# A diffusion transformer's first phase: three modulation mixtures move from TensorE to GpSimd and to the head of the queue

## The chip, the cores and the metric

The kernel runs on one core of a Trainium2 chip. The metric is the device time of one execution in microseconds (us), from the first to the last instruction with the little that lies around them; the time before is the median of three executions. TensorE is called PE here, VectorE DVE, ScalarE ACT, GpSimd POOL and SyncE SP, as in the profile. SP does no arithmetic in this kernel: it issues most of the transfers, in its program order, so that a transfer whose buffer isn't free holds up all that stand behind it.

## The reference, cut to what matters

The kernel computes a two-layer backbone. Layer 0 is a neighbourhood attention followed by a mixture of experts, layer 1 a bidirectional RWKV-7 mixing followed by another mixture of experts. Width is 1024, with 512 latent and 256 context tokens. Every layer is steered by six modulation vectors (shift, scale and gate for the mixer, the same for the experts):

```python
def ada_modulation(cond, w, b):
    m = jax.nn.silu(cond) @ w + b
    return jnp.split(m, 6, axis=-1)
```

`w` is 1024 x 6144 float32 for each layer, so each of the twelve modulations reads a 4 MB slice of weights and multiplies it with one or two vectors (`c` for the latent tokens and `c_ctx` for the context tokens). The three that the change touches, j = 3, 4, 5 of layer 1, steer the last mixture of experts, which is used for latent tokens alone.

## The kernel before, in words

Four phases follow one another: layer 0's attention (0 to about 500 us), its experts (to about 1190), the RWKV mixing (to about 2130), the last experts (to the end). The change lies in the first phase, `phase_na`.

**Start.** Six 128-row tiles of tokens are loaded and normalised, TensorE turns them to channels-first form (`raw`), and the two modulations j = 0 and 1 of layer 0 are computed. Then, for each of 8 chunks of channels k and for two column ranges (512 latent, 256 context), ACT writes the modulated tokens rounded to a shorter format, `hTh` (L563), and DVE writes the modulated tokens in full (`raw`, L564) and what the rounding lost, `hTl` (L566). These 32 DVE instructions are called the hTl chain here. At the same time POOL clears the two `kl` tiles (L230) and makes the attention masks `mR` with six selects (L237).

**The weave.** From then on a generator interleaves three lists of steps: the attention of one pair of heads (`na_attend`: scores L362, L363 and mask L372; softmax; transposes L80; values L411), the projection of the next pair (`na_project`: products in three passes L262, L263, L264 with weights `wraw` loaded by SP at L275, rounded by ACT to `wh` at L254, and the rest taken by DVE to `wl` at L255; POOL copies half of `kT` at L327), and the remaining modulations, `mods`, by `ADA` steps for each pair of heads, 33 of 40 in all. The other 7 steps run at the end, beside the last attention steps. The programming layer then orders each engine's queue by its own rules; each engine, and each queue of transfers, works strictly in order.

**One modulation, `ada(S, l, j)`.** Four steps. Each loads 256 rows of weights, 1 MB, into a buffer `adaw` (L129, SP, two buffers). TensorE multiplies: 8 matmuls of 128x256 by the vector's 32-column tile `sT` (L133; columns 0 and 1 carry the two vectors), and in the first step 4 small matmuls that add the bias `adab` (L138; loaded by POOL's queue at L126). DVE copies (L140) or adds (L142) the sum into `adam`. After four steps two transposes (L80) and a DVE copy (L147) write the column form `modT`. `adam` and `adab` have two buffers each.

Every float32 matmul appears as two records in the trace, so a step's 8 matmuls are 16 records of L133.

The order of the modulations was layer 0, j = 2 to 5, then layer 1, j = 0 to 5.

Of the kernel before, what the change touches and what calls it, by code (L numbers as in the profile page):

```python
# [20 lines left out]
F32 = mybir.dt.float32  # L21
# [5 lines left out]
ALU = mybir.AluOpType  # L27
# [4 lines left out]
P = 128  # L32
D = 1024
# [17 lines left out]
def vap(ap, dims, offset=0):  # L51
    return bass.AP(tensor=ap.tensor, offset=ap.offset + offset, ap=dims)
# [25 lines left out]
def transpose(S, out, in_):  # L78
    n = in_.shape[0]
    S.nc.tensor.transpose(out, in_, S.ident[:n, :n])  # L80
# [37 lines left out]
    S.modT = [cp.tile([P, 48, 2], F32, name=f"modT{l}") for l in range(2)]  # L118


def ada(S, l, j):

    nc, I = S.nc, S.I
    acc = S.small.tile([P, 256], F32, name="adam")
    adab = S.small.tile([24, 256], F32, name="adab")
    nc.gpsimd.dma_start(adab, I["ada_b"][l].rearrange("(c n) -> c n", n=256))  # L126
    for k in range(0, KD, 2):
        w = S.adaw.tile([P, 2, D], F32, name="adaw")
        nc.sync.dma_start(w, I["ada_w"][l, k * P:(k + 2) * P, j * D:(j + 1) * D].rearrange("(i p) n -> p i n", p=P))  # L129
        ps = S.ps_mm.tile([P, 512], F32, name="mm")[:, :256]  # L130
        for i in range(2):
            for q in range(4):
                nc.tensor.matmul(ps[32 * q:32 * q + 32], S.sT[:, k + i, :], w[:, i, q * 256:(q + 1) * 256],  # L133
                                 start=i == 0, stop=i == 1 and k > 0)
        if k == 0:
            for q in range(4):
                c = 4 * j + q
                nc.tensor.matmul(ps[32 * q:32 * q + 32], S.ident[0:24, c:c + 1].to_broadcast([24, 32]),  # L138
                                 adab, start=False, stop=True)
            nc.vector.tensor_copy(acc, ps)  # L140
        else:
            nc.vector.tensor_tensor(acc, ps, acc, op=ALU.add)  # L142
        yield
    pt = S.ps_tp.tile([P, 4, P], F32, name="tp")
    for s in range(2):
        transpose(S, pt[:, s, :], acc[:, s::2] if l == 1 and j in (3, 4) else acc[:, s * P:(s + 1) * P])
    nc.vector.tensor_copy(S.modT[l][:, 8 * j:8 * j + 8, :].rearrange("p (q s) w -> p s q w", s=2),  # L147
                          pt[:, 0:2].rearrange("p s (q r) -> p s q r", r=32)[:, :, :, 0:2])
# [73 lines left out]
def na_consts(S, pool):  # L222
    nc = S.nc
    S.mL = pool.tile([P, P], BF16, name="mL")
    nc.vector.memset(S.mL, 0.0)
    nc.vector.tensor_copy(S.mL[0:16].rearrange("m (c r) -> m c r", r=GR),
                          S.ident[0:16, 0:16, None].to_broadcast([16, 16, GR]))
    S.kl = [pool.tile([P, 2, 768], F32R, name=f"kl{i}") for i in range(2)]
    for i in range(2):
        nc.gpsimd.memset(S.kl[i].bitcast(F32), 0.0)  # L230
    S.mR = []
    for t in range(3):
        m = pool.tile([P, 32, GR], BF16, name=f"mR{t}")
        nc.vector.memset(m, 0.0)

        def sel(lo, hi, base, cm, step):
            nc.gpsimd.affine_select(out=m[0:16, lo:hi, :], in_=m[0:16, lo:hi, :],  # L237
                                    pattern=[[step, hi - lo], [0, GR]], compare_op=ALU.is_ge,
                                    fill=NEG, base=base + step * lo, channel_multiplier=cm)
        if t == 0:  # L240
            sel(0, 32, 8, -1, 1)
            sel(16, 32, 7, 1, -1)
        elif t == 1:
            sel(0, 32, 0, -1, 1)
            sel(0, 32, 15, 1, -1)
        else:
            sel(0, 16, -8, -1, 1)
            sel(0, 32, 23, 1, -1)
        S.mR.append(m)
# [17 lines left out]
def split_weights(S, pool, tag, sources, bufs):  # L267

    nc = S.nc
    out = []  # L270
    for h in range(2):
        raw = S.wraw.tile([P, 4, 256], F32, name="wraw")
        for c, src in sources:
            n = src.shape[1]
            nc.sync.dma_start(raw[:, :, c:c + n], src[h * 512:(h + 1) * 512].rearrange("(k p) n -> p k n", p=P))  # L275
        wh = pool.tile([P, 4, 256], F32R, name=f"{tag}h", bufs=bufs)
        wl = pool.tile([P, 4, 256], F32R, name=f"{tag}l", bufs=bufs)
        split(S, wh, wl, raw)
        out.append((wh, wl))
    return lambda k: tuple(w[:, k % 4, :] for w in out[k // 4])  # L280


def na_project(S, p, hT, wp, grp, Q):

# [3 lines left out]
    def product(w, t):  # L288
        ps = S.ps_mm.tile([P, 2, 256], F32, name="mm")
        for i in range(2):  # L290
            s = slice((t + i) * P, (t + i + 1) * P)
            passes(S, ps[:, i, :], [(hTh[:, k, s], hTl[:, k, s]) + w(k) for k in range(KD)])
            yield ps
    Q.q = grp.tile([P, 2, 768], F32R, name="qT")
    Q.k = grp.tile([P, 2, 768], F32R, name="kT")
    Q.kl = S.kl[p % 2]
    Q.BT = grp.tile([P, 2, 265], F32, name="BT")
    for s in range(2):
        nc.sync.dma_start(Q.BT[:, s], vap(S.rp, [[1, 16], [31, 8], [1, 265]], 465 * (2 * p + s)))
    w = split_weights(S, wp, "w", [(i * P, W[:, i * D + p * P:i * D + (p + 1) * P]) for i in range(2)], 3)  # L300
# [218 lines left out]
def phase_na(S):  # L519
    nc, tc, I = S.nc, S.tc, S.I  # L520
    with ExitStack() as es:
        pool = es.enter_context(tc.tile_pool(name="na", bufs=1))
# [34 lines left out]
        for j in range(2):  # L557
            for _ in ada(S, 0, j):
                pass
        cols = [mod_cols(S, 0, w, 0) for w in range(2)]  # L560
        for k in range(KD):
            for (a, b), sl in zip(cols, (slice(0, 512), slice(512, 768))):
                nc.scalar.activation(hTh[:, k, sl], raw[:, k, sl], AF.Identity, scale=a[:, k:k + 1], bias=b[:, k:k + 1])  # L563
                nc.vector.tensor_scalar(raw[:, k, sl], raw[:, k, sl], a[:, k:k + 1], b[:, k:k + 1],  # L564
                                        op0=ALU.mult, op1=ALU.add)
# [3 lines left out]
        grp = ea.enter_context(tc.tile_pool(name="nag", bufs=2, side="right", reuse_waits="tile"))  # L569
        att = ea.enter_context(tc.tile_pool(name="naa", bufs=1, side="right", reuse_waits="tile"))  # L570
        na_consts(S, att)
        Q = [Ctx() for _ in range(8)]

        def modulation():
            for l, js in ((0, range(2, 6)), (1, range(6))):
                for j in js:
                    yield from ada(S, l, j)
        def attention():
            for p in range(8):
                yield from na_attend(S, p, Q[p], Q[p - p % 2].V, Q[p - p % 2].VS, OT)  # L580

        def some(gen, n):
            for _ in range(n):
                next(gen, None)
                yield
        mods, att = modulation(), attention()
        weave(1, (na_project(S, 0, (hTh, hTl), wp, grp, Q[0]), 0, 1))
        for p in range(7):
# [1329 lines left out]
def phase_rw(S):  # L1918
    nc, tc = S.nc, S.tc
    S.rwk = ExitStack()  # L1920
    with ExitStack() as es:
        pool = es.enter_context(tc.tile_pool(name="rw", bufs=1))
        with ExitStack() as e1:
            if S.first == 3:
                with tc.tile_pool(name="adat", bufs=4) as S.adaw:
                    S.small = S.adaw
                    for j in range(6):
                        for _ in ada(S, 1, j):
                            pass
            S.small = e1.enter_context(tc.tile_pool(name="smallr", bufs=2))  # L1930
            rw_consts(S, pool)
            rw_inputs(S, pool)
# [4 lines left out]
        with ExitStack() as e1:  # L1937
# [56 lines left out]
            for k in range(n + LAG + 1):  # L1994
                j = k - LAG
# [47 lines left out]
def build(tc, I, out, upto=99, dbg=None, xin=None, first=1):  # L2043
    with ExitStack() as ctx:
# [28 lines left out]
        if upto >= 3:  # L2073
            R = phase_rw(S)
            if upto == 3:
                R.es.close()
# [40 lines left out]
```

## Time and profile before

| | |
|---|---|
| median of three runs | 2639.2 us (2630.35 to 2642.72) |
| profiled execution, its own time | 2646.59 us |
| its span, first to last instruction | 2644.8 us |
| PE busy, share of the span | 2400.1 us, 91% |
| DVE | 1275.4 us, 48% |
| ACT | 982.8 us, 37% |
| POOL | 555.3 us, 21% |
| mean granted TensorE clock | 0.954 of full speed |

A share is an average over four phases. The stretch of the first phase has to be read by itself, and within it three things: who waits for whom on PE, what each record of the modulations costs there, and what DVE and POOL do at the same moments. Where the trace shows a group such as "x16", the time beside it runs from the first start to the last end of the group. "[0.38 <-PE mm L264]" at the end of a row is idle time of that engine before the instruction and what ended it; "SPq" is SP's queue, and the time there is that of issuing, not of the transfer. In a line with three durations these are the shortest, the median and the longest, in ns.

### The profile page before, as it was taken

Reading aid. Unit: us, or ns where it says so; the run is one execution under the profiler, and the core shown is the slowest. Engines: PE = TensorE matmul, PEld = TensorE weight load, DVE = VectorE, ACT = ScalarE, POOL = GpSimd, SP = SyncE. Lnnn points to the kernel's source line nnn. Section 1 sums busy time; section 2 is a strip of 40 time slices with the busy share of each in tenths; the row PEclk is TensorE's granted clock in tenths of the full one; section 3 lists DMA queues with packets and bytes.
Section 4 is the critical chain, followed back from the end, with each engine's and each line's share of the span. In section 5 each row is a group of like instructions: output and inputs, shape, how many; then the busy total and the mean of one; then the engine's idle time right before and its main releaser. Section 6 shows DMA issues by size and latency. Waiting matters only on the chain. (4 is left out here: it accounts for less than half of the span.)

```text
span 2644.8 us, 43708 instructions
## 1 busy us (share of the span) xinstructions
PE 2400.1 (91%) x16800; PEld 1565.9 (59%) x16800; DVE 1275.4 (48%) x2997; ACT 982.8 (37%) x2057; POOL 555.3 (21%) x831
## 2 busy tenths in 40 slices
PE   5999999988999999996997979999999959998887
PEld 3988888783333433334896868777778843332232
DVE  5666666552222322339777445767666751222122
ACT  3566565431111111114676435666664421011010
POOL 2110100120000000005354055556565200000000
PEclk9999999998999999998997988989998959999999
DMA  6344444437989999863678665565553189999998
GB/s 249 99 130 143 139 131 137 163 147 294 409 352 365 367 350 378 320 239 121 184 244 281 172 137 117 127 131 130 128 125 97 59 333 403 420 421 420 420 421 342
DMA packets 402334, 637.59 MB, mean 241 GB/s; under 512 B 133220, under 2 KB 300448, under 8 KB 377552
## 3 DMA queue, kind: packets, MB, share of 16 engines
q1 hardware_dynamic: 395200, 613.30, 66.3%
q0 software_dynamic: 6928, 21.51, 2.2%
q8 instruction: 133, 2.18, 0.3%
q14 instruction: 73, 0.60, 0.1%
HBM read 565.11 MB, written 53.88 MB: 234 GB/s over the span
## 5 line engine op out<-in xcount | busy, mean ns | idle before, releaser
L823 PE MATMUL P<-wm,xin 128*64 128x512 f32 x2048 | 469.5, 601 | 25.6 <-DMA wm<-in_moe_w_dram 24.3
L823 PEld LDWEIGHTS P<-wm,xin 128*64 128x64 f32 x2048 | 140.4, 137 | 318.6 <-issue 251.3
L869 PE MATMUL mm<-wm,hidT 128*64 128x512 f32 x1024 | 233.7, 604 | 9.2 <-ACT hidT L856 7.1
L879 DVE SCALAR_TENSOR_TENSOR Y<-mm,gates,gt 64x512 f32<-64x512 f32 x64 | 48.0, 750 | 329.4 <-PE mm L869 328.7
L841 ACT ACTIVATE hid<-P 128x512 f32<-128x512 f32 x32 | 19.1, 597 | 443.9 <-PE P L823 443.9
L798 POOL DMA_INDIRECT xg<-xnd,ii x20 | 19.1, 953 | 775.9 <-PE tp L80 718.1
L262 PE MATMUL mm<-wh,hTh 128*128 128x256 f32 x576 | 168.1, 292 | 2.1 <-ACT hTh L563 2.1
L264 PE MATMUL mm<-wh,hTl 128*128 128x256 f32 x576 | 166.3, 289 | 1.6 <-DVE hTl L566 1.6
L263 PE MATMUL mm<-wl,hTh 128*128 128x256 f32 x576 | 165.8, 288 | 0.0
L869 PEld LDWEIGHTS mm<-wm,hidT 128*64 128x64 f32 x1024 | 71.1, 138 | 154.6 <-issue 134.8
L1648 POOL TENSOR_TENSOR Wi<-Wi,Ti 112x30 f32<-112x30 f32 (+14 forms) x240 | 141.7, 591 | 18.8
L1646 POOL TENSOR_TENSOR Ti<-Wi 112x30 f32<-112x30 f32 (+14 forms) x240 | 136.8, 570 | 18.2
L842 DVE TENSOR_TENSOR hid<-P,hid 128x512 f32<-128x512 f32 x32 | 22.1, 692 | 243.4 <-PE P L823 228.3
L832 PE MATMUL Pc<-wm,xin 128*32 128x512 f32 x1024 | 118.2, 603 | 0.0
L1725 PE MATMUL mm<-FR,QF 128*128 128x128 f32 (+1 forms) x768 | 117.5, 299 | 0.4 <-ACT QF L1713 0.4
L262 PEld LDWEIGHTS mm<-wh,hTh 128*128 128x128 f32 x576 | 110.7, 192 | 8.2 <-issue 5.7
L264 PEld LDWEIGHTS mm<-wh,hTl 128*128 128x128 f32 x576 | 110.6, 192 | 4.3 <-DVE hTl L566 2.7
L263 PEld LDWEIGHTS mm<-wl,hTh 128*128 128x128 f32 x576 | 110.7, 192 | 2.6 <-issue 2.5
L1725 PEld LDWEIGHTS mm<-FR,QF 128*128 128x128 f32 x768 | 101.0, 204 | 7.4 <-ACT QF L1713 0.9
L1713 ACT ACTIVATE QF<-mm 64x256 f32<-64x256 f32 x192 | 72.6, 378 | 69.3 <-PE mm L1709 65.6
L1728 DVE TENSOR_TENSOR FT<-mm,eye 64x128 f32<-64x128 f32 x192 | 55.9, 292 | 82.5 <-ACT FT L1727 80.4
L1742 PE MATMUL ch<-Z,FT 128*64 128x64 f32 x704 | 81.5, 241 | 9.2 <-DVE Z L1745 7.5
(445 smaller groups left out, 5542.1 us busy)
## 6 DMA issues: line engine op xcount, KB each, us to landing
wm<-in_moe_w_dram SPq DMA_DIRECT2D x382, 1024.0 KB
adaw<-in_ada_w_dram SPq DMA_DIRECT2D x48, 1024.0 KB
wraw<-in_na_w_qkv_dram SPq DMA_DIRECT2D x32, 256.0 KB
pkd<-sig SPq DMA_DIRECT2D x24, 256.0 KB
pkd<-kka SPq DMA_DIRECT2D x24, 256.0 KB
pkd<-av SPq DMA_DIRECT2D x24, 256.0 KB
sig<-pkd SPq DMA_DIRECT2D x16, 384.0 KB
kka<-pkd SPq DMA_DIRECT2D x16, 384.0 KB
```

The lines of the kernel that those rows point to most:

```text
L262: S.nc.tensor.matmul(ps, xh, wh, start=(k == 0), stop=False)
L263: S.nc.tensor.matmul(ps, xh, wl, start=False, stop=False)
L264: S.nc.tensor.matmul(ps, xl, wh, start=False, stop=(k == n - 1))
L823: S.nc.tensor.matmul(ps[64 * hf:64 * hf + 64], T.xl[:, k, T.cl], w[:, hf * 512:(hf + 1) * 512], start=k == 0, stop=k == KD - 1)
L832: S.nc.tensor.matmul(T.Pc[32 * i:32 * i + 32], T.xc[:, k, T.cc], w[:, (i % 2) * 512:(i % 2 + 1) * 512], start=k == 0, stop=k == KD - 1)
L869: S.nc.tensor.matmul(py[64 * hf:64 * hf + 64], T.hT[:, k % 4, k // 4, :], weights(R, "moe_w2", T.e, k)[:, hf * 512:(hf + 1) * 512], start= ...
L1646: nc.gpsimd.tensor_tensor(t, W3[:, i + 1:32, i:i + 1].to_broadcast([112, n, i]), W3[:, i:i + 1, 0:i].to_broadcast([112, n, i]), op=ALU.mult)
L1648: nc.gpsimd.tensor_tensor(W3[:, i + 1:32, 0:i], W3[:, i + 1:32, 0:i], t, op=ALU.add)
L1713: nc.scalar.activation(QF[m][0:64, u], pq[64 * u:64 * u + 64], AF.Copy)
L1725: nc.tensor.matmul(pf[:, h, s0:], QF[m][:, u, h, :], rhs, start=True, stop=True)
L1728: nc.vector.tensor_tensor(F[64:128, :, 64:128], pf[64:128, :, 64:128], S.eye2[64:128, None, :].to_broadcast([64, 2, 64]), op=ALU.add)
L1742: nc.tensor.matmul(pz[64:128, h, :], FT[m][u][:, h, 64:128], Zs[m][:, u, 64 * h:64 * h + 64], start=True, stop=True)
```

## The change

For layer 1, j = 3, 4, 5, POOL takes each 128-row slice of the weights, multiplies it by its entry of the vector (one number for each partition) and adds it to a sum `adas` of 128x1024, which has one buffer: 8 multiplications (the first one writes `adas`, L145; the others write in place, L147) and 7 additions (L148) for each modulation. TensorE then sums `adas` over the partitions with a tile of ones: 4 matmuls (L168) and the 4 bias matmuls (L171), and DVE copies the result (L172). The transposes and the copy to `modT` stay. These three modulations now come first of the ten woven ones, ahead of layer 0's. `adam` and `adab` get one buffer instead of two. The lines below are otherwise unchanged and moved down: L129 is L140, L133 is L154, L138 is L159, L254 and L255 are L283 and L284, L262 to L264 are L291 to L293, L275 is L304, L327 is L356, L362 and L363 are L391 and L392, L411 is L440, L564 and L566 are L593 and L595.

```diff
+def ones(S, pool):
+    S.sums = pool
+    S.one = pool.tile([P, 32], F32, name="one", bufs=1)
+    S.nc.vector.memset(S.one, 1.0)

 def ada(S, l, j):
-    acc = S.small.tile([P, 256], F32, name="adam")
-    adab = S.small.tile([24, 256], F32, name="adab")
+    acc = S.small.tile([P, 256], F32, name="adam", bufs=1)
+    adab = S.small.tile([24, 256], F32, name="adab", bufs=1)
     nc.gpsimd.dma_start(adab, I["ada_b"][l].rearrange("(c n) -> c n", n=256))
+    if l == 1 and j > 2:
+        sums = S.sums.tile([P, D], F32, name="adas", bufs=1)
     for k in range(0, KD, 2):
         w = S.adaw.tile([P, 2, D], F32, name="adaw")
         nc.sync.dma_start(w, ...)
+        if l == 1 and j > 2:
+            for i in range(2):
+                s = S.sT[:, k + i, 0:1]
+                if k + i == 0:
+                    nc.gpsimd.tensor_scalar(sums, w[:, i], s, None, op0=ALU.mult)
+                else:
+                    nc.gpsimd.tensor_scalar(w[:, i], w[:, i], s, None, op0=ALU.mult)
+                    nc.gpsimd.tensor_tensor(sums, sums, w[:, i], op=ALU.add)
+            yield
+            continue
         ps = S.ps_mm.tile([P, 512], F32, name="mm")[:, :256]
...
         yield
+    if l == 1 and j > 2:
+        ps = S.ps_mm.tile([P, 512], F32, name="mm")[:, :256]
+        for q in range(4):
+            nc.tensor.matmul(ps[32 * q:32 * q + 32], S.one, sums[:, q * 256:(q + 1) * 256], start=True, stop=False)
+        for q in range(4):
+            c = 4 * j + q
+            nc.tensor.matmul(ps[32 * q:32 * q + 32], S.ident[0:24, c:c + 1].to_broadcast([24, 32]), adab, start=False, stop=True)
+        nc.vector.tensor_copy(acc, ps)
     pt = S.ps_tp.tile([P, 4, P], F32, name="tp")
...
         na_consts(S, att)
+        ones(S, att)
...
-            for l, js in ((0, range(2, 6)), (1, range(6))):
+            for l, js in ((1, range(3, 6)), (0, range(2, 6)), (1, range(3))):
```

POOL's queue at the start, before: the bias loads of later modulations, the clears, the six selects, then the first copies of `kT`.

```order
L126 DMA adab<-in_ada_b_dram 24x256 x2
L230 MEMSET kl_430 128x1536
L230 MEMSET kl_431 128x1536
L237 AFFINE_SELECT mR_434<-mR_434 16x256
L237 AFFINE_SELECT mR_442<-mR_442 16x256
L237 AFFINE_SELECT mR_450<-mR_450 16x128
L237 AFFINE_SELECT mR_434<-mR_434 16x128
L237 AFFINE_SELECT mR_442<-mR_442 16x256
L237 AFFINE_SELECT mR_450<-mR_450 16x256
L327 CAST kT<-kT 64x256 x3
```

The same place of the changed kernel, from the clears on (two bias loads and three multiplications stand ahead of it):

```order
L145 TENSOR_SCALAR adas<-adaw,sT 128x1024
L266 AFFINE_SELECT mR_434<-mR_434 16x256
L266 AFFINE_SELECT mR_442<-mR_442 16x256
L266 AFFINE_SELECT mR_450<-mR_450 16x128
L148 TENSOR_TENSOR adas<-adas,adaw 128x1024
L266 AFFINE_SELECT mR_434<-mR_434 16x128
L266 AFFINE_SELECT mR_442<-mR_442 16x256
L266 AFFINE_SELECT mR_450<-mR_450 16x256
L148 TENSOR_TENSOR adas<-adas,adaw 128x1024 x2
L147 TENSOR_SCALAR adaw<-adaw,sT 128x1024 x2
L148 TENSOR_TENSOR adas<-adas,adaw 128x1024
L147 TENSOR_SCALAR adaw<-adaw,sT 128x1024 x2
```

Ahead of the first copy of `kT` POOL now has four multiplications and four additions among and behind the selects.

The second of the three modulations, j = 4 of layer 1, at its end. `adas_1533` is its sum, `adaw_1976` its last chunk of weights; `adaw_2122` is the first chunk of the next modulation and `adas_2121` that one's sum. POOL's queue of the changed kernel:

```order
L148 TENSOR_TENSOR adas_1533<-adas_1533,adaw_1976 128x1024
L147 TENSOR_SCALAR adaw_2122<-adaw_2122,sT_105 128x1024
L148 TENSOR_TENSOR adas_1533<-adas_1533,adaw_1976 128x1024
L145 TENSOR_SCALAR adas_2121<-adaw_2122,sT_105 128x1024
L135 DMA adab_2119<-in_ada_b_dram 24x256
```

The last addition to `adas_1533` stands behind a multiplication that needs `adaw_2122`. SP's queue of the changed kernel around that chunk:

```order
L140 DMA adaw_1976<-in_ada_w_dram 128x2x1024
L304 DMA wraw_2722<-in_na_w_qkv_dram 128x4x128 x2
L328 DMA BT_2144<-rpbp_130 128x1x265 x2
L304 DMA wraw_2729<-in_na_w_qkv_dram 128x4x128 x2
L140 DMA adaw_2122<-in_ada_w_dram 128x2x1024
L304 DMA wraw_3074<-in_na_w_qkv_dram 128x4x256
L140 DMA adaw_2191<-in_ada_w_dram 128x2x1024
```

`adaw_2122` is behind four loads of `wraw`, each of which needs a buffer of `wraw` that DVE's `wl` has read. TensorE's queue where this sum is taken, before (the modulation that stood near this place was one of layer 0, on TensorE):

```order
L362 MATMUL sc<-kT,qT 128x256
L363 MATMUL sc<-kl_431,qT 128x256
L80 MATMUL tp<-ident,sb 128x128 x2
L411 MATMUL po<-PT,V 64x128 x8
L80 MATMUL tp<-ident,adam 128x128 x2
L133 MATMUL mm<-adaw,sT 32x256 x8
L138 MATMUL mm<-adab,ident 32x256 x4
```

and in the changed kernel, where between the values and the ones-matmuls there also come three groups of scores:

```order
L391 MATMUL sc<-kT,qT 128x256
L392 MATMUL sc<-kl_430,qT 128x256
L440 MATMUL po<-PT,V 64x128 x4
L401 LDWEIGHTS mL
L401 MATMUL sc<-mR_442,mL 128x256
L391 MATMUL sc<-kT,qT 128x256
L392 MATMUL sc<-kl_430,qT 128x256
L391 MATMUL sc<-kT,qT 128x256
L392 MATMUL sc<-kl_430,qT 128x256
L168 MATMUL mm<-adas,one 32x256 x4
L171 MATMUL mm<-adab,ident 32x256 x4
L291 MATMUL mm<-wh,hTh 128x256
```

All products of the next projection (L291 on) stand behind the ones-matmuls.

The third of them, j = 5 of layer 1, and the first chunk of the modulation after it (layer 0, j = 2, on TensorE again, chunk `adaw_2564`). TensorE's queue of the changed kernel:

```order
L391 MATMUL sc<-kT,qT 128x256
L392 MATMUL sc<-kl_430,qT 128x256
L168 MATMUL mm<-adas,one 32x256 x4
L171 MATMUL mm<-adab,ident 32x256 x4
L154 MATMUL mm<-adaw,sT 32x256 x8
L80 MATMUL tp<-ident,adam 128x128 x2
L80 MATMUL tp<-ident,sb 128x128 x4
L154 MATMUL mm<-adaw,sT 32x256 x8
L291 MATMUL mm<-wh,hTh 128x256
```

and SP's queue of the changed kernel around `adaw_2564`:

```order
L140 DMA adaw_2425<-in_ada_w_dram 128x2x1024
L328 DMA BT_2719<-rpbp_130 128x1x265 x2
L304 DMA wraw_3080<-in_na_w_qkv_dram 128x4x256
L304 DMA wraw_3475<-in_na_w_qkv_dram 128x4x128 x2
L140 DMA adaw_2564<-in_ada_w_dram 128x2x1024
L140 DMA adaw_2690<-in_ada_w_dram 128x2x1024
```

The first chunk for TensorE is issued behind the loads `wraw_3080` and `wraw_3475`.

## Rows read from the trace of the kernel before

**Rows 1.** Stretches: length, busy PE, PEld, DVE, ACT, POOL, granted clock, DMA share, GB/s.
```profile
52.50:69.00 16.50, 13.07 (x74) 11.45 (x75) 15.42 (x34) 9.70 (x16) 5.42 (x7) 0.79 0.00 1
...
97.00:448.00 351.00, 350.92 (x3234) 297.97 (x3233) 224.07 (x658) 214.16 (x426) 29.82 (x66) 1.00 0.42 131
448.00:500.00 52.00, 47.79 (x452) 34.83 (x452) 38.04 (x106) 35.47 (x71) 2.73 (x5) 0.93 0.66 222
```

**Rows 2.** Waits of PE from 50 to 97 us: us, times, longest us.
```profile
PE mm L262 <- ACT hTh L563: 2.1, 2, 1.7
PE mm L264 <- DVE hTl L566: 1.6, 3, 0.8
```

**Rows 3.** Instructions on the tiles adaw and adab, whole run.
```profile
L133 PE MATMUL mm<-adaw,sT x768: 379/379/637, 16.0 to 488.0; 128*32 128x256 f32 x192
...
L138 PE MATMUL mm<-adab,ident x96: 374/397/632, 35.0 to 474.6; 24*32 24x256 f32 x96
```

**Rows 4.** The tile adaw alone on PE and PEld, 300 to 400 us.
```profile
300.00:400.00 100.00, 11.93 (x160) 4.41 (x160) 1.00 0.44 131
```

**Rows 5.** Timeline of PE at the second early modulation's end.
```profile
49.70 1.07 PE L133 MATMUL mm<-adaw,sT 128*32 128x256 f32 x16
51.32 0.44 PE L80 MATMUL tp<-ident,adam 128*128 128x128 f32 x2 [0.55 <-DVE adam L142]
```

**Rows 6.** Groups of DVE by shape, 52.5 to 69 us: busy us, mean ns.
```profile
L566 DVE TENSOR_TENSOR hTl<-raw,hTh 128x512 fp32r<-128x512 f32 x8 | 6.0, 754 | 0.0
L564 DVE TENSOR_SCALAR raw<-raw,A,B 128x512 f32<-128x512 f32 x8 | 4.6, 575 | 0.8 <-ACT hTh L563 0.8
```

**Rows 7.** Timeline of POOL, 50 to 60 us.
```profile
50.87 2.77 POOL L230 MEMSET kl<- 128x1536 f32 x2 [6.17 <-DMA wraw<-in_na_w_qkv_dram]
53.60 4.32 POOL L237 TENSOR_SCALAR_AFFINE_SELECT mR<-mR 16x256 bf16<-16x256 bf16 x6
```

**Rows 8.** Single lines of POOL, whole run: shortest, median, longest ns.
```profile
L1652 POOL COPY Xi<-Wi x8: 1962/1996/2671, 1557.3 to 2017.7; 112x1024 f32<-112x1024 f32 x8
...
L1242 POOL TENSOR_TENSOR md<-md,hh x8: 1546/1548/2262, 1219.0 to 1262.6; 128x770 f32<-128x770 f32 x8
...
L327 POOL CAST kT<-kT x48: 392/397/1467, 78.8 to 459.1; 64x256 fp32r<-64x256 f32 x48
```

**Rows 9.** Timelines of DVE and POOL where both work at once.
```profile
1215.20 2.49 DVE L255 TENSOR_TENSOR wl<-wraw,wh 128x1024 fp32r<-128x1024 f32 x1
...
1208.00 11.02 POOL L1231 TENSOR_TENSOR xx<-hh 128x770 f32<-128x770 f32 x6
...
81.09 1.21 DVE L255 TENSOR_TENSOR wl<-wraw,wh 128x1024 fp32r<-128x1024 f32 x1
...
81.09 1.47 POOL L327 CAST kT<-kT 64x256 fp32r<-64x256 f32 x1 [1.90 <-ACT kT L322]
```

**Rows 10.** Timelines of DVE, SP and PE, 194 to 198 us.
```profile
194.39 1.23 DVE L255 TENSOR_TENSOR wl<-wraw,wh 128x1024 fp32r<-128x1024 f32 x1 [1.01 <-ACT wh L254]
...
195.64 0.93 SPq L275 DMA_DIRECT2D wraw<-in_na_w_qkv_dram  x2
...
195.08 1.09 PE L411 MATMUL po<-PT,V 128*64 128x128 f32 x16
...
196.47 1.07 PE L133 MATMUL mm<-adaw,sT 128*32 128x256 f32 x16
```

**Rows 11.** One load of adaw: its issue, and the last stretch with traffic.
```profile
253.15 0.37 SPq L129 DMA_DIRECT2D adaw<-in_ada_w_dram  x1
...
257.00:258.00 1.00, 1.00 (x11) 0.96 (x10) 0.51 (x2) 0.06 (x1) 0.00 (x0) 1.00 0.51 201
```

**Rows 12.** Timelines of DVE, SP and PE, 239 to 244 us.
```profile
240.24 1.22 DVE L255 TENSOR_TENSOR wl<-wraw,wh 128x1024 fp32r<-128x1024 f32 x1
...
241.53 2.55 SPq L275 DMA_DIRECT2D wraw<-in_na_w_qkv_dram  x2
...
239.99 1.07 PE L133 MATMUL mm<-adaw,sT 128*32 128x256 f32 x16
```

More of the change, by code (lines that the diff above doesn't have):

```diff
@@ L1926, in phase_rw @@
                     S.small = S.adaw
+                    ones(S, S.adaw)
                     for j in range(6):
```

## The prediction

> **What bounds the kernel now.** I read the busy time by stage first, then TensorE's waits, then the modulations' own rows, then DVE beside POOL. The change stays within the first 500 us, so a time won or lost there is passed on to the phases behind, which follow one another. In the weave, from 97 to 448 us, PE is busy 350.92 of 351.00 us at full granted clock while POOL works only 29.82 us [rows 1]: there the sequence of PE's instructions is the time, each record taken away shortens it, and anything that makes PE wait lengthens it by all of the wait. Before the weave, from 52.5 to 69 us, it is otherwise: DVE is busy 15.42 of 16.5 us and PE 13.07, at a granted clock of 0.79 [rows 1], and PE's waits there name ACT's `hTh` and DVE's `hTl` [rows 2]. That stretch belongs to the hTl chain. So the reader is to see three things: what PE saves, what POOL does to the hTl chain, and where PE will now wait for POOL's sums or for the loads that POOL holds up.
>
> **What PE saves.** In 300 to 400 us the 160 records on `adaw` take 11.93 us of PE, 0.0746 us each [rows 4]; all 48 steps have 768 records, 16 each [rows 3]. A modulation on TensorE has 4 x 16 records and 8 of the bias, 72; on POOL it keeps 8 of the ones and 8 of the bias, 16. Three modulations save 3 x 56 = 168 records, at 0.0746 us 12.5 us. The first start to last end of a chunk overlaps what follows it a little (49.70 + 1.07 is for 16 records [rows 5], yet the next work starts sooner), so I take **-11.5 us**, with bounds of -10 and -12.5. DVE loses 12 accumulations and gains 3 copies, off the path: it has 127 us idle in the weave [rows 1].
>
> **What POOL's work costs by itself.** The trace of before has no such multiplication and no addition of 1024 columns. The nearest rows: a copy of 112x1024 at 1.996 us and an addition of 128x770 at 1.548 us, 2.06 us if scaled to 1024; the smallest by its size is the copy of 64x256 at 0.397 us, 1.6 us scaled [rows 8]. I take 2.0 us for each of the 24 multiplications and 21 additions, the value the two nearest rows agree on, with 1.6 and 2.6 as ends: 90 us of POOL in some 190 us, in a stretch where POOL was nearly idle, so nothing by itself. [...]
>
> **The start.** POOL's queue before holds clears of 2.77 us and six selects of 4.32 us there [rows 7]. Now a multiplication and three additions stand among and behind the selects, and then, as soon as the third chunk lands, two multiplications, an addition and two more multiplications, all ahead of the first copy of `kT`. The hTl chain runs in that time, 32 DVE instructions of 0.42 to 0.75 us, the widest at 754 and 575 ns [rows 6]. How the two engines meet is shown where both work on wide tiles: DVE's `wl` took 2.49 us beside POOL's six additions (11.02 us) against 1.21 us elsewhere, and in another place it was the POOL copy that took 1.47 us [rows 9] where its median is 0.397 [rows 8]. One of the two loses, by about 1.28 us of DVE for each POOL operation. Four operations are certain to fall into the chain, nine may; with seven I get 7 x 1.28 = **+9 us**. Ends: 3 us (if a collision costs half of that and only four fall in) and 18 us (nine operations at 2.0 us, DVE wholly blocked). PE follows the chain almost one to one, since the last chunk of `hTl` closes the first products. [...]
>
> With one buffer of `adam`, the second early modulation's first accumulation waits for the first one's transposes. PE's transposes already wait 0.55 us for `adam` at 51.32 [rows 5]; I put this at **+1 us** (0 to 2).
>
> **The second sum (j = 4).** POOL's last addition stands behind a multiplication that needs the next modulation's first chunk, and SP issues that chunk behind loads of `wraw` that wait for DVE's `wl`. In the times of before: `wl` ends at 194.39 + 1.23 = 195.62, SP issues two `wraw` loads from 195.64 for 0.93 us [rows 10], then the chunk at 196.6. From issue to landing it takes 4.5 to 5 us (issued at 253.15, traffic into the stretch 257 to 258 [rows 11]), so it lands at about 201.4; a multiplication and an addition of 2.0 us make the sum ready at 205.4. PE has its values behind it at 196.2 (195.08 + 1.09 [rows 10]). The three groups of scores and values put between take some 2.3 us (10 score products, 3 masks and 8 records of values, at about 0.12 us apart), so it comes to the ones-matmuls at 198.5. All products of the next projection queue behind them. **+7 us** (4 to 9). The first sum, j = 3, is done by about 110 us and wanted 40 us later: nothing.
>
> **After the third sum (j = 5).** POOL ends at about the time when PE asks. The wait is for the chunk behind it: `wl` ends at 240.24 + 1.22 = 241.46, SP issues `wraw` from 241.53 [rows 12] and the chunk at about 242.4, landing at 247. PE comes there at about 239.6, where in the times of before it was doing a chunk already in place, at 239.99 [rows 12]. That is 7.4 us, and the second chunk, whose two buffers POOL held equally long, lands 2.5 us after the first while PE has 1.5 us of other work: **+8 us** (4 to 10). Before, two TensorE chunks were always loaded ahead, so this wait is new.
>
> From 448 us on the order is that of before, with seven steps left.
>
> **The sum.** -11.5 + 9 + 1 + 7 + 8 = **+13.5 us**, on the profiled execution's 2646.6 us 2660.1. That execution is 7.4 us above the median of the runs, 2639.2, on which the forecast is 2652.7 us. A measurement of this kernel can tell about 0.5%, 13.2 us, from no change: the forecast stands just at that line.
>
> **The rivals.**
>
> *Half prices.* A collision on DVE costs less and the chunks are issued earlier, since DVE has lost its accumulations: start 3, `adam` 1, waits 3 each. -11.5 + 10 = -1.5 us: 2637.7. For it: the six selects of 4.32 us [rows 7] lie beside a DVE that still reaches 15.42 of 16.5 us [rows 1]. Against it: the wide rows [rows 9].
>
> *Cover holds everywhere.* The sums end before PE asks and the hTl chain isn't touched. Its place is the landing of `adaw_2122` and `adaw_2564`; it decides where SP issues them about 7 us sooner than I have it, because PE, 11.5 us ahead in all and having put other work first, releases `wraw` sooner. Then only the saving is left: 2627.7 us, not slower. Against it: SP's issue at 195.64 comes 0.02 us after `wl` [rows 10], so the queue really waits for that.
>
> *DVE is blocked for the whole of each POOL operation.* Seven operations then cost 7 x 2.0 = 14 us in place of 9, and the sum is +18.5: 2657.7 us. For it: a POOL copy that met a `wl` lasted until that was over (81.09 + 1.47 against 81.09 + 1.21 [rows 9]), so one does block the other wholly. Against it: `wl` lost 1.28 us beside additions of 1.84 us each (11.02 / 6 [rows 9]). [...]
>
> [...]
>
> That the change doesn't do what it says, because PE isn't the bound, is excluded by 350.92 of 351 us [rows 1].
>
> **How the numbers follow.** Forecast 0.4, half prices 0.2, cover 0.1, blocked DVE 0.15, falling clock 0.15. Half of the forecast's case lies above 2652.4, the line of 0.5%, and most of the last two: 0.2 + 0.12 + 0.14 = 0.46 for slower. Faster by over 0.5% needs below 2626.0, the cover case with a saving of 12.5 us and a little more: 0.06. Within: 0.48. The range goes from 2629, which leaves out most of the cover case, to 2668, which takes in the clock case and a start of 18 us with waits at their upper ends.
>
> **What would show it.** Right: in the changed profile DVE's L593 and L595 rows longer at 52 to 80 us, with POOL's L145 and L148 beside them; a wait of PE at the ones-matmuls L168 for POOL of about 7 us, once; a wait at L154 for the transfer `adaw` of 7 to 8 us, once; 576 records of L154 in place of 768, and 24 of L168. Wrong: no waits of PE in the weave, or multiplications on POOL of 1 us or of 4 us; and if the weave's end comes later than the sum of these terms, the clock in the rows behind each wait will tell.

## The result, and the profile after

The changed kernel takes **2677.8 us** (median of four runs, 2673.04 to 2683.07) against 2639.6 before: a ratio of 1.0158, 95% interval 1.0138 to 1.0178. It is slower by some 38 us where 2652.7 was forecast, and lies outside the range of 2629 to 2668. The direction was right, the size was not.

The profiled execution took 2673.36 us with a span of 2671.6, only 26.8 us longer than the profiled one of before. The rest is seen when the same instruction's start is compared in the two traces. I call the difference of these starts the **lag**. For the n-th product record (L262 before, L291 after; both have 1376 in this phase and later) it is +18.3 us where that record stood at 92 us, +13.8 at 151, +24.7 at 209, +41.6 at 273, +41.9 at 401, +39.0 at 507 and +38.6 at 1270. So the loss is made by 273 us and passed on. In the RWKV phase, which the change doesn't touch, the two executions then differ by some 12 us the other way (+40.6 at 1514, +26.8 at 2130); the lag near 507 us agrees with the medians, and I use it below.

Stages of the changed kernel (columns as in [rows 1]):

```profile
52.50:69.00 16.50, 4.33 (x14) 3.07 (x14) 15.60 (x16) 9.68 (x16) 16.42 (x12) 0.50 0.25 71
69.00:97.00 28.00, 23.17 (x143) 21.51 (x144) 20.62 (x32) 3.53 (x8) 12.79 (x5) 0.76 0.18 54
97.00:150.00 53.00, 52.21 (x441) 49.24 (x440) 38.68 (x94) 34.50 (x66) 23.77 (x21) 1.00 0.35 101
200.00:250.00 50.00, 39.00 (x314) 34.26 (x310) 26.27 (x63) 19.50 (x39) 28.73 (x16) 0.86 0.34 108
250.00:300.00 50.00, 37.09 (x316) 27.98 (x314) 27.55 (x59) 22.15 (x46) 22.60 (x14) 0.83 0.42 134
300.00:350.00 50.00, 49.93 (x472) 42.68 (x471) 30.57 (x87) 30.10 (x61) 5.80 (x12) 1.00 0.46 137
```

Three stretches have lost PE time: the start, 200 to 250 and 250 to 300. In the first one DVE is busy 15.60 us as before, but with 16 instructions instead of 34 [rows 1], and PE has 14 records instead of 74. PE's waits from 40 to 560 us (us, times, longest):

```profile
PE mm L168 <- POOL adas L148: 17.4, 2, 9.4
PE mm L293 <- DVE hTl L595: 14.6, 7, 6.4
...
PE mm L154 <- DMA adaw<-in_ada_w_dram: 2.4, 1, 2.4
```

The wait for `hTl` was 1.6 us [rows 2]. The two waits for POOL's sums are new.

**The start.** Timelines of DVE, then of POOL, in the changed kernel:

```profile
56.78 4.26 DVE L595 TENSOR_TENSOR hTl<-raw,hTh 128x512 fp32r<-128x512 f32 x1
60.96 7.56 DVE L593 TENSOR_SCALAR raw<-raw,A,B 128x512 f32<-128x512 f32 x3
68.45 1.01 DVE L595 TENSOR_TENSOR hTl<-raw,hTh 128x512 fp32r<-128x512 f32 x2
...
70.65 1.58 DVE L593 TENSOR_SCALAR raw<-raw,A,B 128x256 f32<-128x256 f32 x2
...
73.42 2.56 DVE L595 TENSOR_TENSOR hTl<-raw,hTh 128x256 fp32r<-128x256 f32 x1
...
58.14 2.34 POOL L148 TENSOR_TENSOR adas<-adas,adaw 128x1024 f32<-128x1024 f32 x1
...
62.43 4.82 POOL L148 TENSOR_TENSOR adas<-adas,adaw 128x1024 f32<-128x1024 f32 x2
67.23 6.12 POOL L147 TENSOR_SCALAR adaw<-adaw,sT 128x1024 f32<-128x1024 f32 x2
73.33 2.37 POOL L148 TENSOR_TENSOR adas<-adas,adaw 128x1024 f32<-128x1024 f32 x1
```

While POOL adds (L148), DVE gets next to nothing done: the subtraction at 73.42, 0.41 us alone, takes 2.56 beside the addition at 73.33, and from 62.43 to 67.23, through two additions, DVE finishes one instruction. (The 4.26 us at 56.78, for 0.68 alone, are one addition of 2.34 and some 1.4 us of POOL's selects ahead of it.) While POOL multiplies (L147, 67.23 to 73.35) it is different: DVE's two subtractions at 68.45 take 1.01 us together, as they do undisturbed, and of the two multiplications at 70.65 the first, of 256 columns, takes 1.12 instead of 0.40 and the second, of 512 columns, its usual 0.53. The groups of DVE from 52 to 90 us, against [rows 6]:

```profile
L593 DVE TENSOR_SCALAR raw<-raw,A,B 128x512 f32<-128x512 f32 x8 | 10.8, 1347 | 0.8 <-ACT hTh L592 0.8
L595 DVE TENSOR_TENSOR hTl<-raw,hTh 128x512 fp32r<-128x512 f32 x8 | 9.0, 1127 | 0.0
L593 DVE TENSOR_SCALAR raw<-raw,A,B 128x256 f32<-128x256 f32 x8 | 7.7, 972 | 0.0
L595 DVE TENSOR_TENSOR hTl<-raw,hTh 128x256 fp32r<-128x256 f32 x8 | 5.4, 680 | 0.0
```

Together 32.9 us where the same groups were 17.5 us before (6.0 + 4.6 [rows 6], and 3.6 + 3.3 for the narrow ones): **+15.4 us** of the lag of 18.3. Another 2.2 us come ahead of the chain, which begins at 55.61 instead of 53.43: PE waits 2.3 us at L154 for DVE's copy into `adam` (L161), which takes 1.67 us instead of 0.42 beside POOL's clear of `kl`, and the two instructions that write `A` take 1.05 us instead of 0.24 beside the first multiplication. POOL's own prices are higher than I took (whole run: shortest, median, longest ns):

```profile
L147 POOL TENSOR_SCALAR adaw<-adaw,sT x21: 2832/2881/3253, 30.0 to 255.4; 128x1024 f32<-128x1024 f32 x21
...
L148 POOL TENSOR_TENSOR adas<-adas,adaw x21: 2328/2394/3434, 58.1 to 268.4; 128x1024 f32<-128x1024 f32 x21
```

The multiplication by one number for each partition, one input, is the dearer one: 2.88 us against 2.39.

**The second sum.** Timelines of POOL, SP and PE:

```profile
200.68 2.42 POOL L148 TENSOR_TENSOR adas<-adas,adaw 128x1024 f32<-128x1024 f32 x1
216.66 2.84 POOL L147 TENSOR_SCALAR adaw<-adaw,sT 128x1024 f32<-128x1024 f32 x1 [13.55 <-DMA adaw<-in_ada_w_dram]
219.48 2.33 POOL L148 TENSOR_TENSOR adas<-adas,adaw 128x1024 f32<-128x1024 f32 x1
...
208.81 0.50 SPq L140 DMA_DIRECT2D adaw<-in_ada_w_dram  x1
...
221.86 1.08 PE L168 MATMUL mm<-adas,one 128*32 128x256 f32 x8 [9.44 <-POOL adas L148]
...
224.26 0.41 PE L292 MATMUL mm<-wl,hTh 128*128 128x256 f32 x1
```

This is the predicted chain: the chunk is issued at 208.81, which is the forecast 196.6 plus a lag of 12.2, lands at 216.66, and a multiplication and an addition later PE goes on. The landing took 7.9 us where I had 4.5 to 5. The products behind the wait then run at 0.41 us each and 0.21 apart instead of 0.28 and 0.12, until 229 us: the granted clock was 0.57 from 215 to 220 us, while PE waited, and 0.50 from 220 to 229 us, when it went on.

**The third sum.** POOL, then PE:

```profile
223.15 2.84 POOL L145 TENSOR_SCALAR adas<-adaw,sT 128x1024 f32<-128x1024 f32 x1 [1.34 <-PE mm L168]
...
262.68 8.04 POOL L148 TENSOR_TENSOR adas<-adas,adaw 128x1024 f32<-128x1024 f32 x3
...
270.76 1.08 PE L168 MATMUL mm<-adas,one 128*32 128x256 f32 x8 [7.98 <-POOL adas L148]
...
275.22 1.93 PE L154 MATMUL mm<-adaw,sT 128*32 128x256 f32 x16 [2.37 <-DMA adaw<-in_ada_w_dram]
```

`adas` has one buffer, so this sum couldn't begin before PE had read the last one, at 223.15. POOL needs 8 x 2.88 + 7 x 2.39 = 39.8 us for a sum, and was done 47.6 us later, at 270.72; the rest lies mostly at the copies of `kT` in its queue, one of which came after 5.5 us without work (at 243.10). The granted clock around the two waits (columns as in [rows 1]):

```profile
215.00:220.00 5.00, 0.00 (x0) 0.00 (x0) 0.00 (x0) 0.00 (x0) 3.34 (x2) 0.57 0.20 71
225.00:230.00 5.00, 5.00 (x28) 5.00 (x28) 0.59 (x4) 0.35 (x1) 4.45 (x4) 0.56 0.27 104
265.00:270.00 5.00, 0.00 (x0) 0.00 (x0) 4.14 (x5) 0.00 (x0) 4.84 (x3) 0.50 0.47 132
275.00:280.00 5.00, 4.78 (x38) 2.33 (x38) 0.61 (x3) 1.26 (x2) 0.00 (x0) 0.50 0.60 195
280.00:285.00 5.00, 5.00 (x52) 3.70 (x45) 2.98 (x9) 2.36 (x7) 0.51 (x1) 0.94 0.96 347
```

### The profile page after: what moved, and what is told of

The parts are those of the page before. It is cut to its first block, busy times and chain, and to the rows that moved or that the text cites. A ratio compares the mean times of both kernels' runs of the same rounds, so it can differ in the third digit from the quotient of the medians.

```text
span 2671.6 us, 43415 instructions
## 1 busy us (share of the span) xinstructions
PE 2387.1 (89%) x16632; PEld 1557.6 (58%) x16632; DVE 1312.9 (49%) x2989; ACT 986.1 (37%) x2061; POOL 676.0 (25%) x876
## 5 line engine op out<-in xcount | busy, mean ns | idle before, releaser
L293 PE MATMUL mm<-wh,hTl 128*128 128x256 f32 x576 | 169.1, 294 | 14.6 <-DVE hTl L595 14.6
L291 PE MATMUL mm<-wh,hTh 128*128 128x256 f32 x576 | 170.9, 297 | 2.2 <-ACT hTh L592 2.2
L293 PEld LDWEIGHTS mm<-wh,hTl 128*128 128x128 f32 x576 | 112.5, 196 | 18.6 <-DVE hTl L595 16.7
L291 PEld LDWEIGHTS mm<-wh,hTh 128*128 128x128 f32 x576 | 113.4, 197 | 8.6 <-issue 5.6
```

The costliest lines, as they stand in the source:

```text
L291: S.nc.tensor.matmul(ps, xh, wh, start=(k == 0), stop=False)
L293: S.nc.tensor.matmul(ps, xl, wh, start=False, stop=(k == n - 1))
```

## The experiments

The lag at three places (the products that stood at 92, 273 and 507 us in the kernel before), from each run's own trace, with the ratio to the kernel before from the timed rounds:

| kernel | lag at 92 | at 273 | at 507 | median, us | ratio (95%) |
|---|---|---|---|---|---|
| the change | +18.3 | +41.6 | +39.0 | 2677.8 | 1.0158 (1.0138 to 1.0178) |
| order only | -0.5 | -0.3 | -0.7 | 2633.2 | 0.9978 (0.9951 to 1.0004) |
| one TensorE modulation first | -0.2 | +9.4 | +29.9 | 2665.9 | 1.0103 (1.0049 to 1.0157) |
| sums not read | +17.9 | +28.0 | +25.1 | 2660.1 | 1.0084 (1.0058 to 1.0109) |
| alternating | +0.7 | -6.3 | +12.3 | 2651.7 | 1.0069 (1.0044 to 1.0094) |
| multiplications on ACT | +19.9 | +14.1 | +11.5 | 2646.0 | 1.0033 (1.0013 to 1.0054) |
| alternating, multiplications on ACT | +1.0 | 0.0 | +1.8 | 2636.5 | 1.0013 (0.9997 to 1.0029) |
| first sum early, others alternating | +19.6 | +29.5 | +31.8 | 2671.9 | 1.0149 (1.0115 to 1.0182) |
| one sum alone | +1.1 | +12.1 | +9.3 | 2645.1 | 1.0043 (1.0022 to 1.0064) |
| no work on POOL | +2.8 | -5.2 | -7.7 | 2630.8 | 0.9967 (0.9944 to 0.9990) |
| no work on POOL, alternating | -0.1 | -9.0 | -12.0 | 2626.9 | 0.9946 (0.9922 to 0.9970) |
| no additions | +13.6 | +6.3 | +3.6 | 2635.3 | 0.9971 (0.9945 to 0.9998) |

**Order only.**

```diff
-    if l == 1 and j > 2:
+    if False:
```

(in all three places)

> The changed kernel with all modulations on TensorE again: only the order (layer 1's j = 3, 4, 5 first) and the single buffers of adam and adab stay. Theory A (the loss of 39 us by 510 us comes from POOL's work alone: the hTl chain blocked at the start, about +18, then two waits for sums with a lower clock behind them, +12 and +18, less the saving): 0 to +3 us against the kernel before, 2639 to 2643 us; no wait of PE in the weave. Theory B (the order and the single buffers themselves cost, by transfers that queue otherwise and by accumulations that wait for transposes): +8 us or more, 2648 us and up, with waits of PE for adam or adaw.

Lag -0.3 to -0.7 throughout: theory A. The order and the single buffers cost nothing by themselves; what follows comes with POOL's work.

**One TensorE modulation first.**

```diff
-            for l, js in ((1, range(3, 6)), (0, range(2, 6)), (1, range(3))):
+            for l, js in ((0, (2,)), (1, range(3, 6)), (0, range(3, 6)), (1, range(3))):
```

> The changed kernel with layer 0's j = 2 (on TensorE) put ahead of the three sums, so that POOL multiplies and adds nothing while the hTl chain runs. Theory A (blocked DVE at the start is +18 of the loss, and independent of the later waits): the hTl chain ends near 69 us as before, the two waits for sums stay about as long, 2678 - 17 = 2661 us (2655 to 2666). Theory C (POOL's pace sets when the third sum is done, so that a later start of POOL comes back as longer waits at the ones-matmuls): 2670 us or more, with waits for sums of 25 us and up in all in place of 17.4.

In between: the time lies at the top of A's range, the waits are C's. The start's lag is gone, but PE waits 27.9 us for sums in three places (17.4 in the change). Of the 18.3 us that it saves at the start, half comes back: the lag at 507 us is 9.1 less than the change's.

**Sums not read.**

```diff
-            nc.tensor.matmul(ps[32 * q:32 * q + 32], S.one, sums[:, q * 256:(q + 1) * 256], start=True, stop=False)
+            nc.tensor.matmul(ps[32 * q:32 * q + 32], S.one, S.sT.rearrange("p k w -> p (k w)"), start=True, stop=False)
```

> The changed kernel with the ones-matmuls reading the constant vector tile in place of the sum; POOL computes the sums as before but nobody reads them (three modulations of layer 1 are left wrong by that). Start unchanged. Theory A1 (the two waits are waits for the last addition only): the 17.4 us of waits and the slower clock behind them go, 2678 - 28 = 2650 us (2646 to 2654). Theory A2 (behind the third sum stands POOL's hold on the two weight buffers, so PE then waits at the next chunk, L154, in place of the ones-matmuls): only the first of the two goes, 12 us, and a few of the other, 2661 us (2656 to 2667), with a load wait at L154 of 8 us or more where it was 2.4.

2660 us, A2's number, and the lag falls to +9.4 at 209 us, where the change had 24.7: the second sum's 12 us were the wait. That is all that comes back. From 209 to 273 us the lag still grows, by 18.6 us where it was 16.9, so the wait for the third sum's last addition isn't by itself what that place costs. A2's reason for it is right only in part, since the load wait is 3.9 us and not 8. Near 250 to 275 us PE now waits like this (`OT` is the result of an attention step):

```profile
PE mm L154 <- DMA adaw<-in_ada_w_dram: 3.9, 1, 3.9
PE po L440 <- DVE OT L443: 3.5, 1, 3.5
```

and runs at a granted clock of 0.50 from 255 to 265 us and 0.51 from 270 to 275. PE's queue has no products left in that place, only attention steps that depend on ACT and DVE. How much of this third loss is POOL's hold on DVE and how much its hold on the weight buffers, this run doesn't separate, and no other does; the kernels below in which POOL has less to do for a sum lose far less here.

**Alternating.**

```diff
-            for l, js in ((1, range(3, 6)), (0, range(2, 6)), (1, range(3))):
+            for l, js in ((0, (2,)), (1, (3,)), (0, (3,)), (1, (4,)), (0, (4,)), (1, (5,)), (0, (5,)), (1, range(3))):
```

> The three sums alternate with layer 0's modulations on TensorE (j = 2 of layer 0, 3 of layer 1, 3 of layer 0, 4 of layer 1, and so on), so that POOL has some 90 us for each. Theory A (POOL's pace of 5.2 us for each 128 rows, 42 us a sum, is what PE waits for when sums follow one another): waits for sums under 3 us each, no blocked start, the saving of 11.5 us stays: 2632 to 2645 us. Theory D (the two shared weight buffers are the limit: TensorE's chunks are loaded late because POOL holds the buffers): load waits at L154 of 5 us or more, three times, 2655 to 2670 us.

Neither. Waits for sums are 2.6 us and for loads 1.3, yet the lag is +12.3 with 11.5 saved. The largest of its waits is another, that of the mask products (L372 before) for the softmax's `nm`:

```profile
PE sc L401 <- DVE nm L411: 7.2, 7, 1.9
```

The softmax on DVE is late. Its groups from 97 to 448 us say why. Before, alternating, and alternating without POOL's work (below), one fence each (L391, L420 and L413 are one line of the three kernels):

```profile
L391 DVE TENSOR_SCALAR sb<-sb,sm 128x512 f32<-128x512 f32 x56 | 27.5, 491 | 1.5
```

```profile
L420 DVE TENSOR_SCALAR sb<-sb,sm 128x512 f32<-128x512 f32 x53 | 39.2, 739 | 1.5
```

```profile
L413 DVE TENSOR_SCALAR sb<-sb,sm 128x512 f32<-128x512 f32 x56 | 27.5, 490 | 1.3
```

What I had seen at the start alone happens in the weave too: on average 0.25 us more for a scaling of the softmax, on the way from scores to values. The average hides how: 34 of the 53 take their usual 0.48 to 0.50 us, and the longest stand beside an addition, as here (alternating kernel, DVE, then POOL):

```profile
278.42 2.52 DVE L420 TENSOR_SCALAR sb<-sb,sm 128x512 f32<-128x512 f32 x1
...
278.31 2.35 POOL L148 TENSOR_TENSOR adas<-adas,adaw 128x1024 f32<-128x1024 f32 x1
```

Nor does the loss come evenly. Record by record, the lag of this kernel less that of the same order without POOL's work rises by 12 us from 177 to 198 us, by 16 from 274 to 282 and by 12 from 362 to 368 (times of the kernel before), once near the end of each sum, and is level or falls in between. From 270 to 300 us of its own time, around the second of these places, the granted clock is 0.83, so here too a slower clock adds to the waits.

**Multiplications on ACT**, in the change's order and in the alternating one.

```diff
-                    nc.gpsimd.tensor_scalar(sums, w[:, i], s, None, op0=ALU.mult)
+                    nc.scalar.activation(sums, w[:, i], AF.Copy, scale=s)
...
-                    nc.gpsimd.tensor_scalar(w[:, i], w[:, i], s, None, op0=ALU.mult)
+                    nc.scalar.activation(w[:, i], w[:, i], AF.Copy, scale=s)
```

> The changed kernel with the 24 multiplications on ACT (one activation with a scale for each 128 rows) and only the 21 additions on POOL. Theory P (a POOL addition blocks the hTl chain for its whole 2.4 us, a POOL multiplication of 2.85 us only slows DVE's multiplications to about half and leaves its subtractions alone; and POOL's 42 us for each sum is what the later waits are made of): the lag at the start falls from 18 us to that of four additions, 8 to 11 us; POOL needs 19 us for each sum, so the wait for the third sum is gone and that for the second, which hangs on a late load, is shorter by 2 us: 2655 to 2664 us. Theory Q (both kinds of POOL work block alike, in proportion to their time): lag at the start 7 us or less. Theory R (the waits come from the late loads and from the order, not from POOL's pace): the sum of the two later lags stays near 30 us, 2665 us or more.

R falls: with POOL's sum at some 17 us (7 x 2.39) neither wait for sums is left, and the lag goes down after the start instead of up. The later waits were POOL's pace. P's time was 9 us too high, and its lag at the start too low: 19.9. Seven additions met DVE there: two ahead of the hTl chain, in front of the small operations that start it (PE's first wait for `hTh` is 7.6 us), one on its first instruction and four after 71.9 us.

> The alternating order (a modulation on TensorE, a sum, a modulation on TensorE and so on) with the multiplications on ACT and the additions on POOL. Theory P: no collision at the start, POOL with 19 us for each sum never late, half as much blocked DVE: the lag near 500 us falls from the 12 us of the alternating kernel to -5 to +5 us, 2634 to 2646 us. Theory S (what is left of the loss there is made by the order of PE's queue and the loads, which the split doesn't change, and ACT's 25 us more cost the softmax): 2648 to 2656 us.

Theory P. Within the uncertainty this one equals the kernel before; it is the best of the versions that compute everything, and no gain. The softmax's scaling takes 553 ns in it. The additions alone still cost 13.8 us of lag (1.8 + 12.0, against the same order without POOL's work below).

**First sum early, others alternating.** The order is (1,3), (0,2), (1,4), (0,3), (1,5), (0,4), (0,5), (1,0) to (1,2) as (layer, j).

> The first sum at the head of the queue as in the change, the other two alternating with TensorE's modulations as in the alternating kernel (2652 us). Theory T (the blocked start is a cost by itself, which nothing later gives back): lag of 16 to 18 us at 92 us and a result 14 to 18 us above the alternating kernel's, 2665 to 2670 us. Theory U (the later waits absorb it, since POOL is ahead of PE after it): 2650 to 2660 us.

Theory T, with 2671.9 us a little above its range: +19.6 at the start and still 19.5 above the alternating kernel's lag at 507.

**One sum alone.** `if l == 1 and j == 5`, in the order (0,2), (0,3), (1,5), (0,4), (0,5), (1,0) to (1,4).

> Only j = 5 of layer 1 goes through POOL, after two of layer 0's modulations on TensorE and ahead of two others; j = 3 and 4 of layer 1 are on TensorE again. Saving of PE 3.8 us. Theory V (each sum costs what a third of the alternating kernel's loss is: 13 us above the kernel before with 11.5 saved, so about 8 us a sum): about +4 us, 2640 to 2646 us. Theory W (the cost comes from sums that crowd on POOL and on the two weight buffers, one alone is nearly free): 2632 to 2638 us.

Theory V by its time, but its 8 us a sum are too few: the lag of +9.3 with 3.8 saved makes 13 us for this one. A single sum waits too: 3.6 us at L168 and 3.0 for a load.

**No work on POOL**, in both orders. The eight multiplications and seven additions of each sum are taken out and the ones-matmuls read the constant tile as above.

> The change with POOL's multiplications and additions left out and the ones-matmuls reading a constant tile (three modulations of layer 1 are left out by that); the weights are still loaded, the order and PE's shorter modulations stay. It measures the saving by itself. Theory X (PE's saving of 11.5 us is real and the rest of the change's +39 us is POOL's): 2624 to 2630 us, lag of -10 to -13 us at 500 us. Theory F (the chunks of modulation matmuls were work without dependences that covered the softmax; with them gone PE waits for ACT and DVE instead): 2631 to 2640 us, with 5 us or more of new waits for PT, nm or sb.

> The same without POOL's work, in the alternating order. Theory X: 2624 to 2630 us, as in the change's order; then the +13 us of the alternating kernel is 25 us of POOL's doing, and the +1 us of the one with the multiplications on ACT is 12 us of it. Theory F: 2631 to 2640 us, waits for ACT and DVE spread over the three places where a modulation now has only its ones-matmuls.

Theory X in the alternating order: -12.0 us at 507. In the change's order -7.7, and 2630.8 us lies between the ranges of X and F; none of F's new waits is there, but at the start PE waits 3.0 us for a load of `adaw`, which the change doesn't. The saving of 11.5 us is there. POOL's work costs 24 us in the alternating order (12.3 + 12.0) and 47 us in the change's (39.0 + 7.7).

**No additions.**

```diff
-                    nc.gpsimd.tensor_tensor(sums, sums, w[:, i], op=ALU.add)
```

(and the ones-matmuls read the constant tile)

> The change with POOL's 24 multiplications of 2.85 us but without the 21 additions, the ones-matmuls reading a constant tile (three modulations of layer 1 left out). Counterpart to the kernel that kept only the additions on POOL, whose lag was 19 us at the start. Theory P (additions block the hTl chain wholly, multiplications only slow DVE's own multiplications to half and leave its subtractions alone): lag of 4 to 8 us at 92 us, later waits small since POOL needs 23 us a sum, 2630 to 2640 us. Theory Q (both block in proportion to their time): lag of 12 to 16 us at 92 us, 2640 to 2650 us.

The lag at 92 us is in Q's range, but not for Q's reason; the time, 2635.3 us, is in P's. The groups of DVE, 52 to 90 us (L592 is L593 here, L594 is L595):

```profile
L592 DVE TENSOR_SCALAR raw<-raw,A,B 128x512 f32<-128x512 f32 x8 | 10.5, 1314 | 0.8 <-ACT hTh L591 0.8
L592 DVE TENSOR_SCALAR raw<-raw,A,B 128x256 f32<-128x256 f32 x8 | 7.0, 882 | 0.0
L594 DVE TENSOR_TENSOR hTl<-raw,hTh 128x512 fp32r<-128x512 f32 x8 | 5.4, 678 | 0.0
```

The wide subtractions take 678 ns, no more than undisturbed, while the multiplications take 1314 in place of 575. One of those eight, of 2.58 us, lies beside POOL's two clears of `kl`, which fall into the chain here; the other seven take 1.13 us on average. So P's two kinds are right, and its size was wrong: DVE's own multiplications take 9.6 us more in all, 2 of them beside the clears, and the rest of the 13.6 isn't taken apart here.

## Why the prediction was wrong, step by step

- **What bounds the kernel, and what PE saves: right.** -11.5 us; measured -12.0 in the alternating order without POOL's work.
- **The price of a POOL operation: too low, and it failed in three terms.** I took 2.0 us for both kinds with ends of 1.6 and 2.6. The multiplication takes 2.88 us, outside the ends, the addition 2.39. The nearest row, a plain copy at 1.996 us [rows 8], is no multiplication by a column of numbers, and the addition of 770 columns, 2.06 us when scaled, came out at 2.39. POOL's busy time rose by 120.7 us (676.0 against 555.3), not 90. Of the two kinds it is the one with one input that is the dearer here.
- **The start: right mechanism, the term +9 is +15.4 in the chain and +18.3 with what lies around it.** I priced a collision by operations at 1.28 us, from additions of 1.84 us. The same row read by time is 1.28 / 1.84 = 0.7 us of DVE for each us of POOL. Nine operations fell into the chain, five multiplications and four additions, 24.6 us with their durations there (12.2 + 2.9 + 9.5), and 0.7 of that is 17 us. So the row would have given the right size, with the right durations and count, but by luck: 0.7 is a mean of two kinds that the row doesn't tell apart. Beside the additions the chain lost all of their time, beside the multiplications about 0.4 of it (5.5 us beside 13). What I named as a rival, DVE blocked wholly, is true beside additions (2.56 us for a subtraction of 0.41); beside multiplications it holds for none of DVE's subtractions (678 ns for one of 512 columns in the kernel without additions, as undisturbed).
- **Behind the start, POOL's work isn't free.** "90 us of POOL ..., so nothing by itself" is the step that failed most plainly. I looked at the collision in one place and not in the weave, where DVE's `wl` and the softmax's scaling meet POOL for 90 us more. Alternating, with hardly a wait for a sum, this and its consequences still take back 24 us.
- **The second sum: right place, right chain, +7 is +12.** The wait is 9.4 us (landing 7.9 us and not 5, dearer POOL operations), and nearly 3 us of half clock follow it: 21 products 0.21 us apart instead of 0.12, and ahead of them the 16 records of ones and bias in 2.0 us instead of some 1.2.
- **The third sum: wrong link.** "POOL ends at about the time when PE asks" put the wait for this sum at nothing without a working, and without counting that `adas` has one buffer. POOL began when PE had read the second sum, already late, and needed 47.6 us; PE waited 8.0 us for the sum and 2.4 for the load I had named for 7 to 8. The half clock behind it (granted 0.50 from 264 to 280 us) shows in the two chunks of 1.93 and 1.94 us instead of 1.07. The lag grew by 17 us here where I had 8. Nor is the wait for the sum the whole of it: with the sums unread the lag grows by 18.6 us in the same place, with the multiplications on ACT by 1.9. What costs is the time that POOL needs for a sum; how much of it reaches PE through the last addition, the weight buffers or DVE, the runs don't separate.
- **The rivals were taken one at a time.** Falling clock, blocked DVE and longer waits all have one cause, POOL's time for an operation, so they came together (with the multiplications on ACT, where both waits are gone, the granted clock was 1.00 from 200 to 300 us). The top of the range, 2668, took a blocked start with the waits' upper ends, but no half clock beside them and nothing for the weave. No run shows the term from which the falling clock's 0.14 and its place in the range follow; the runs showed a granted clock of 0.50 behind both waits, which behind the second sum cost nearly 3 us.
- The `adam` term of +1 us: in the order-only kernel, which has the single buffers, PE waits 0.8 us for the copy into `adam` (L161) and the lag at 92 us is -0.5, so it costs nothing there. In the change that wait is 2.3 us, because the copy takes 1.67 us instead of 0.42 beside POOL's clear, and the last early chunk starts 1.3 us later (51.03 against 49.70 [rows 5]).

## What to carry to other kernels

An operation moved to POOL isn't free because POOL is idle (POOL's work cost 24 us here in the alternating order and 47 in the change's): look first at whether DVE works at the same time, and price the move, for each kind of operation by itself, by POOL's time multiplied by what DVE loses in each us (at the start of the change about 1 us beside additions and 0.4 beside multiplications), in all the stretches where both run, not only where DVE is the bound. A sum with one buffer chains the next sum's start to the reader of the last one (223.15 us here), so its wait is to be worked out from the reader's time and not from the loads. And where several rivals hang on one unknown price, the range has to hold them together.

## What the runs showed of the hardware

- Beside POOL's additions of two 128x1024 tiles (2.39 us each, the change) DVE's multiplications and its two-input subtractions were held alike: one of 256 columns each took 2.42 us instead of 0.40 and 2.56 instead of 0.41.
- In the kernel without additions, beside POOL's multiplications of one such tile by a column (2.85 us each) and its selects, DVE's subtractions of 512 columns took 678 ns on average. Seven of its eight multiplications of 512 columns took 0.53 to 1.61 us, 1.13 on average, instead of 0.53.
- In the same kernel the eighth took 2.58 us beside two POOL clears, 2.72 us together.
- In the change the granted clock was 0.50 behind each of the two waits of 9.4 and 8.0 us, for some 7 and 10 us of PE's work; behind the second sum this made the wait cost nearly a third more than its length.
